# Scan chunk tiles in the place that the level tiles leave, one head group of a hybrid encoder layer

## The chip, the core and the metric

One core of a Trainium2 chip runs one program. Its engines work side by side, each through a queue of its own in a fixed order: TensorE (PE) multiplies, VectorE (DVE), ScalarE (ACT) and GpSimd (POOL) do the elementwise work, and SyncE (SP) issues every DMA of this kernel, one after the other. The metric is the time of one execution on the device in microseconds (us). A profiled execution gives the time of every instruction.

## What is computed

One layer of a bidirectional encoder on 1024 tokens of width 1024, all in float32. Cut to the parts that matter here:

```python
proj = h @ w_in[l]                      # columns for attention, delta net, gate, decays
aq, ak, av, dqkv, dgate, dalpha, dbeta = jnp.split(proj, IN_SPLITS, axis=-1)
attn_o = _window_attention(aq, ak, av, attn_sink[l])     # 8 heads, +-128 tokens
dn_o = _gated_deltanet(dqkv, dgate, ...)                 # 4 heads, both directions
mix = jnp.concatenate([attn_o, dn_o], axis=-1) @ w_out[l]
x = x + _rms_norm(mix, g_mix_post[l])
...                                     # cross-attention into 256 memory tokens, SwiGLU

def step(state, inp):                   # inside the delta net: the scan over chunks
    qg_i, kg_i, u_i, w_i, qk_i, gl_i = inp
    v_new = u_i - jnp.einsum('bhck,bhkv->bhcv', w_i, state)
    o_i = jnp.einsum('bhck,bhkv->bhcv', qg_i, state) + jnp.einsum('bhij,bhjv->bhiv', qk_i, v_new)
    state = state * gl_i[..., None, None] + jnp.einsum('bhck,bhcv->bhkv', kg_i, v_new)
    return state, o_i
```

## The kernel before

**Stages.** The program is a chain of stages. Lists of short codes give the order in which their pieces are written; a scheduler then orders the instructions on each engine when the program is built, and each engine runs them in that order. ORDER_1 projects keys, queries and values of the delta net, convolves them and prepares their chunk products. ORDER_2 (line 38) holds the attention projections (A, V), the gate projections (G), the levels (L, one for each of the four delta-net heads) and the first attention windows (W). ORDER_3 (line 39) holds the norm of the memory tokens (M), the scan steps of both head groups (s01), windows (W), the key products of the memory (K, line 941) and its value products (V, line 954). The output projection `w_out` follows (line 1098), then cross-attention and the feed-forward part.

**Matmuls in three passes.** Weights are loaded as float32 (`wraw`, line 122), cast to a high part on ACT (`whi`, line 103) and subtracted to a low part on DVE or POOL (`wlo`, line 104); three matmuls make one product. `wraw`, `whi` and `wlo` have two buffers each.

**Levels.** `levels(h)` (line 556) solves the triangular systems of one head by blocks. It works in tiles of the pool `tl` (line 743: cz, cw, m5, c5, c6, L5, L6, D5, D6, Z0, Z1, Ul and small ones) and stores Z0 and Z1 to `d_pz` (line 628), from where the scans read them. Two halves of one head run through each other.

**Windows.** `window(n, g)` (line 632) is attention of 128 tokens for four heads: load `qr` (643), scores `psw` on PE (654), the maximum on DVE (656), exponentials on ACT (663), scaling by 1/sum on DVE or ACT (672 or 674); then, in the second half, transposes `ptw` (680), high and low parts `ph` and `pl` (103, 104), the product with the values `pow` (685), and the store of `ao` to `d_mix` (688 to 690). `psw` and `ptw` share two PSUM banks.

**Scans.** `scan(g)` (line 795) is a generator for one head group (two heads, two directions), eight steps. In each step it loads a chunk's `kv` (two DMAs of 512 KB, line 824) and `pz` (two of 256 KB, line 825), multiplies (line 809, PSUM tiles `psc`), makes the corrected values, the new state S and the output `of` or `ol`; the second four steps also load a gate tile and store `osq` to `d_mix` (line 906). The output projection loads `d_mix` as `mraw` (line 1094).

**Where the tiles lie.** Pools are stacks on two sides of the on-chip memory. On the left: `wp` (weights), `sm`, `tw` (windows), then `tl`. On the right: `ra`, then in ORDER_2 the pools of `p1` (`hx` with the normalised input, `trp` with the tiles `rop` and `gt`), and after `p1.close()` (line 787) in the place of these the pool `t3` of the scans (line 793). `tl` is entered in `p1`, so it is closed there, and `mk` (line 914: the memory's norm and its operand `mT`) then stands where `tl` stood. A new tile must wait until the last access to the tiles that lay in its place.

**Chunk tiles.** Even steps ("near") take `pz` from `ra` (tag `rr`) and, for group 0, `kv` from `ra` (tag `sct`). All the rest lies in `t3`: `pz` of the odd steps and `kv` of group 0's odd steps one buffer each, `kv` of group 1 two buffers. A `pz` tile takes 4 KB and a `kv` tile 8 KB of a partition.

Of the kernel before, what the change touches and what calls it, by code (L numbers as in the profile page):

```python
# [10 lines left out]
F32 = mybir.dt.float32  # L11
# [8 lines left out]
P = 128  # L20
# [14 lines left out]


ORDER_1 = ("k0 k1 E0 K0 U0 E1 K1 U1 S0 q0 v0 q1 C0 v1 E2 C1 k2 E3 k3 q2 K2 U2 v2 K3 U3 S1 q3 C2 v3 C3 B0 B1").split()
ORDER_2 = "L0 L1 A4 V A0 A1 G0 G1 L2 L3 W W W A2 A3 G2 G3 W".split()
ORDER_3 = ("M " + "s01 W K " * 5 + "s01 K " * 3 + "s01 V V").split()


# [35 lines left out]
def tile_hybrid_block(  # L77
# [11 lines left out]
    if dump is None:  # L89
        def dump(name, ap):  # L90
            pass
# [17 lines left out]
    def pool(name, bufs, **kw):  # L109
        return tc.tile_pool(name=name, bufs=bufs, reuse_waits="tile", **kw)  # L110
# [26 lines left out]
    p12 = ExitStack()  # L137
# [8 lines left out]
    ra = p12.enter_context(pool("ra", 1, side="right"))  # L146
    p1 = ExitStack()
# [196 lines left out]
    G = sm.tile([P, 2, 4, NT], F32, name="G")  # L344
# [33 lines left out]
    sct = ra.tile([P, 2, S], F32, tag="sct", name="sct")  # L378
# [350 lines left out]
    def issue(order, table):  # L729
        for o in order:  # L730
            table[o[0]](*(int(c) for c in o[1:]))
# [8 lines left out]
    tw = p12.enter_context(pool("tw", 2))  # L740
    tw.tile([P, 384], F32, tag="sc", name="sc", bufs=8)
    vhl = tw.tile([P, NT + 1, 2, 2, 64], F32R, tag="vhl", name="vhl", bufs=1)[:, 0:NT]
    tl_ = p1.enter_context(pool("tl", 2))

    def pair():
        t = ra.tile([P, 2, HALF], F32, tag="rr", name="rr", bufs=2)
# [35 lines left out]
            nc.scalar.activation(gt, pp[hf], AF.Silu)  # L782
            nc.sync.dma_start(d_gate[h * P:(h + 1) * P, hf * HALF:(hf + 1) * HALF], gt)

    issue(ORDER_2, {"A": attn_proj, "V": value_proj, "G": gate_proj, "L": levels, "W": next_windows})
    dump("d_q", d_q); dump("d_k", d_k); dump("d_gate", d_gate)
    p1.close()
    pgs.close()
# [6 lines left out]
    def scan(g):  # L795
# [5 lines left out]
        def tl(name, shape=QUAD, **kw):  # L801
            return t3.tile(shape, F32, tag=f"{name}{g}", name=name, **kw)
# [9 lines left out]
        for step in range(NT):  # L812
# [1 line left out]
            cs = (step, NT - 1 - step)  # L814

            near = step % 2 == 0
            pz = (ra.tile([P, 2, 2, 2, P], F32, tag="rr", name="pz", bufs=2) if near else tl("pz", [P, 2, 2, 2, P], bufs=1))
            if g == 0:
                kv = (ra.tile([P, 2, 2, 4, P], F32, tag="sct", name="kv") if near else tl("kv", [P, 2, 2, 4, P], bufs=1))
            else:  # L820
                kv = tl("kv", [P, 2, 2, 4, P])
            before = loaded
            for d in range(2):
                loaded = nc.sync.dma_start(kv[:, d], d_kv[g][cs[d]])
# [129 lines left out]
    def next_values():  # L954
# [12 lines left out]
        for t in range(2):  # L967
            vv = mk.tile([P, 512], F32, tag="cv", name="vv", bufs=2)
            nc.scalar.copy(vv, pp[t])
            nc.sync.dma_start(d_mv[t, :, ch * 512:(ch + 1) * 512], vv)  # L970

    scans = [scan(g) for g in range(2)]

    def scan_step(pairs):
# [23 lines left out]
    L0 = ExitStack()  # L998
# [84 lines left out]
    L1 = ExitStack()  # L1083
# [29 lines left out]
    L2 = ExitStack()  # L1113
# [63 lines left out]
    L3 = ExitStack()  # L1177
# [13 lines left out]
    def turned_k(xn, k):  # L1191
        pt = pn.tile([P, 512], F32, tag="pn", name="ptn")
        for j in range(4):
            nc.tensor.transpose(pt[:, j * P:(j + 1) * P], xn[j][:, k * P:(k + 1) * P], ident)  # L1194
        return pt
# [8 lines left out]
    for k in range(HK):  # L1204
        p0, p1 = turned_k(xn, k), turned_k(xn, k + HK)
# [32 lines left out]
    for e in range(EARLY):  # L1238
        f = 2 * e
        sg = te.tile([P, 512], F32, tag="sg", name="sg0")  # L1240
        w, A = [], []
# [21 lines left out]
    def bank(name):  # L1263
        return pg.tile([P, 512], F32, tag="pg", name=name)
# [60 lines left out]
    for f in (2 * p for p in turns):  # L1325
# [9 lines left out]
        for i, (W1, W22, (S1, S2, S3, S4), _) in enumerate(wts):  # L1335
            a1, v, u = (tg.tile([P, 512], F32, tag=n, name=n, bufs=b_) for n, b_ in (("a1", 1), ("v", 2), ("u", 1)))
            A = None
            if early:
                nc.sync.dma_start(a1, d_m1[f + i])
            else:  # L1340
                A = bank("pA")
# [10 lines left out]
        for i, (W1, W22, (S1, S2, S3, S4), _) in enumerate(wts):  # L1352
            A, D_, E_, v = st[i]
# [101 lines left out]
    A = [bank("pdA") for _ in range(4)]  # L1455
# [104 lines left out]
```

## Time and profile before

| | |
|---|---|
| runs | 1535.87, 1537.51, 1537.88 us |
| median of the runs | 1537.51 us |
| span of the profiled execution | 1537.6 us |
| PE busy | 1481.4 us (96%), 7451 matmuls |
| DVE busy | 1067.1 us (69%) |
| ACT busy | 743.3 us (48%) |
| POOL busy | 374.6 us (24%) |
| moved by DMA | 242.95 MB, mean 158 GB/s |

The span runs from the first to the last instruction of the profiled execution. A busy share is an average over all stages; a stage has to be read on its own, by a table of its stretch of time or by the instructions in order of time. "Idle before" in such a row is the time for which the engine had nothing to run, and the name after the arrow is what ended it.

### The profile page before, as it was taken

Reading aid. Unit: us, or ns where it says so; the run is one execution under the profiler, and the core shown is the slowest. Engines: PE = TensorE matmul, PEld = TensorE weight load, DVE = VectorE, ACT = ScalarE, POOL = GpSimd, SP = SyncE. Lnnn points to the kernel's source line nnn. Section 1 sums busy time; section 2 is a strip of 40 time slices with the busy share of each in tenths; the row PEclk is TensorE's granted clock in tenths of the full one; section 3 lists DMA queues with packets and bytes.
Section 4 is the critical chain, followed back from the end, with each engine's and each line's share of the span. In section 5 each row is a group of like instructions: output and inputs, shape, how many; then the busy total and the mean of one; then the engine's idle time right before and its main releaser. Section 6 shows DMA issues by size and latency. Waiting matters only on the chain. (4 is left out here: it accounts for less than half of the span.)

```text
span 1537.6 us, 21036 instructions
## 1 busy us (share of the span) xinstructions
PE 1481.4 (96%) x7451; PEld 1246.6 (81%) x7451; DVE 1067.1 (69%) x1732; ACT 743.3 (48%) x1518; POOL 374.6 (24%) x364
## 2 busy tenths in 40 slices
PE   6999999998999899999999999999999999999997
PEld 5888888787999777888888877888888888888786
DVE  6868999686788776534346387776877555696665
ACT  6578732457457665454336564323223333354532
POOL 2020210111247103253102232443433432000021
PEclk9999999999999999999999999999999999999999
DMA  6244575856997665454213354343533334853355
GB/s 207 76 116 139 156 188 155 197 173 166 309 321 219 216 208 195 138 165 136 69 55 138 104 198 130 123 130 110 171 124 96 110 104 161 291 185 96 103 176 166
DMA packets 264710, 242.95 MB, mean 158 GB/s; under 512 B 33801, under 2 KB 203678, under 8 KB 264606
## 3 DMA queue, kind: packets, MB, share of 16 engines
q1 hardware_dynamic: 264605, 241.62, 50.4%
q8 instruction: 58, 0.95, 0.3%
q14 instruction: 47, 0.38, 0.1%
HBM read 172.07 MB, written 66.88 MB: 155 GB/s over the span
## 5 line engine op out<-in xcount | busy, mean ns | idle before, releaser
L103 ACT CAST whi<-wraw 128x1024 fp32r<-128x1024 f32 x108 | 113.4, 1051 | 154.8 <-issue 31.7
L261 PE MATMUL pg<-hlo,whi 128*128 128x512 f32 x352 | 139.5, 397 | 0.0
L261 PE MATMUL pg<-hhi,whi 128*128 128x512 f32 x352 | 139.2, 396 | 0.0
L261 PE MATMUL pg<-hhi,wlo 128*128 128x512 f32 x352 | 138.5, 394 | 0.0
L104 POOL TENSOR_TENSOR wlo<-wraw,whi 128x1024 fp32r<-128x1024 f32 x38 | 91.7, 2414 | 178.7 <-ACT whi L103 169.4
L104 DVE TENSOR_TENSOR wlo<-wraw,whi 128x1024 fp32r<-128x1024 f32 x70 | 87.1, 1245 | 58.6 <-ACT whi L103 54.6
L1052 PE MATMUL pmg<-whi,b 128*128 128x512 f32 x384 | 119.0, 394 | 0.4 <-ACT b L103 0.4
L1231 PE MATMUL pA<-s,whi 128*128 128x512 f32 x352 | 109.3, 392 | 1.0 <-ACT m L1248 1.0
L1052 PEld LDWEIGHTS pmg<-whi,b 128*128 128x128 f32 x384 | 71.4, 188 | 15.3 <-ACT b L103 1.3
L1421 PE MATMUL pdX<-dhl,whi 128*128 128x512 f32 x264 | 76.1, 390 | 1.5 <-ACT dhl L103 0.8
L1231 PEld LDWEIGHTS pA<-s,whi 128*128 128x128 f32 x352 | 65.5, 188 | 14.7 <-ACT m L1248 1.5
L261 PEld LDWEIGHTS pg<-hhi,whi 128*128 128x128 f32 x352 | 66.5, 189 | 13.4 <-ACT hhi L103 0.2
L261 PEld LDWEIGHTS pg<-hhi,wlo 128*128 128x128 f32 x352 | 66.5, 189 | 12.9
L261 PEld LDWEIGHTS pg<-hlo,whi 128*128 128x128 f32 x352 | 66.4, 189 | 12.8
L1052 PE MATMUL pmg<-wlo,b 128*128 128x512 f32 x192 | 71.9, 391 | 0.0
L1308 POOL TENSOR_TENSOR act<-act,up 128x512 f32<-128x512 f32 x33 | 50.1, 1520 | 88.6 <-DVE up L1307 53.2
L103 ACT CAST whi<-araw 128x1024 fp32r<-128x1024 f32 (+1 forms) x36 | 35.4, 982 | 71.4 <-PE pdX L1421 27.6
L1231 PE MATMUL pA<-s,wlo 128*128 128x512 f32 x176 | 68.6, 391 | 0.8 <-DVE wlo L104 0.7
L104 DVE TENSOR_TENSOR wlo<-araw,whi 128x1024 fp32r<-128x1024 f32 (+1 forms) x36 | 40.8, 1133 | 38.5 <-ACT whi L103 38.4
L286 DVE SCALAR_TENSOR_TENSOR acc<-cp,cols,acc 128x1024 f32<-128x1024 f32 x48 | 62.1, 1296 | 0.1
L1280 POOL TENSOR_TENSOR sr<-wraw 128x512 f32<-128x512 f32 x22 | 30.6, 1392 | 127.0 <-DMA wraw<-in_w_gate_up_dram 125.8
L1451 POOL TENSOR_SCALAR frs<-sq 128x1 f32<-128x1 f32 x8 | 12.0, 1497 | 195.9 <-ACT jk L1440 195.0
(415 smaller groups left out, 4097.9 us busy)
## 6 DMA issues: line engine op xcount, KB each, us to landing
wraw<-in_w_gate_up_dram SPq DMA_DIRECT2D x52, 512.0 KB, 3.8
kv<-d_kv SPq DMA_DIRECT2D x32, 512.0 KB, 6.9
wraw<-in_w_in_dram SPq DMA_DIRECT2D x22, 512.0 KB, 5.6
b<-in_w_down_dram SPq DMA_DIRECT2D x20, 512.0 KB, 7.0
araw<-d_as SPq DMA_DIRECT2D x20, 512.0 KB, 3.9
pz<-d_pz SPq DMA_DIRECT2D x32, 256.0 KB, 5.3
wraw<-in_w_ckv_dram SPq DMA_DIRECT2D x16, 512.0 KB, 8.7
wraw<-in_w_out_dram SPq DMA_DIRECT2D x16, 512.0 KB, 4.0
```

The costliest lines, as they stand in the source:

```text
L103: nc.scalar.copy(hi, src)
L104: (eng or nc.vector).tensor_tensor(lo, src, f32(hi), ALU.subtract)
L261: nc.tensor.matmul(p_, w[:, k, :], ah[a][:, k, :], start=(k == 0 and i == 0), stop=(k == nk - 1 and i == 2))
L286: nc.vector.scalar_tensor_tensor(acc, cp[:, t:t + S], taps[t], acc, ALU.mult, ALU.add)
L1052: nc.tensor.matmul(pp[t], act[a][:, k, tt], w_[:, kk, :], start=(k == 0 and i == 0), stop=(k == KT - 1 and i == 2))
L1231: nc.tensor.matmul(out_, w[a][:, k, :], xx[b_][:, k, :], start=(start and k == 0 and i == 0), stop=(k == HK - 1 and i == 2), skip_group_ch ...
L1280: nc.gpsimd.tensor_tensor(s[0], b_[:, 0:HK], b_[:, HK:], ALU.add)
L1308: nc.gpsimd.tensor_tensor(o_, o_, up, ALU.mult)
L1421: nc.tensor.matmul(banks[t], a[:, k - k0, tt], w, start=(first and k == 0 and i == 0), stop=(k == NB - 1 and i == 2), skip_group_check=not ...
L1451: nc.gpsimd.tensor_scalar(rs, sq[:, 1, t:t + 1], sq[:, 0, t:t + 1], D * EPS, ALU.add, ALU.add)
```

## The change

`tl` gets an exit stack of its own and is closed by a new entry T in ORDER_2, written after the levels of the last head. In its place on the left a pool `tk` is opened, which stays until the scans end. `pz` of the odd steps, `kv` of group 0's odd steps and both buffers of `kv` of group 1 now come from `tk` (4 + 8 + 4 + 16 = 32 KB of a partition) and not from `t3`. The number of buffers of each stays the same.

```diff
-ORDER_2 = "L0 L1 A4 V A0 A1 G0 G1 L2 L3 W W W A2 A3 G2 G3 W".split()
+ORDER_2 = "L0 L1 A4 V A0 A1 G0 G1 L2 L3 T W W W A2 A3 G2 G3 W".split()
...
-    tl_ = p1.enter_context(pool("tl", 2))
+    ptl = ExitStack()
+    tl_ = ptl.enter_context(pool("tl", 2))
+    tk = []
+
+    def scan_chunks():
+
+        ptl.close()
+        tk.append(p12.enter_context(pool("tk", 2)))
+
...
-    issue(ORDER_2, {"A": attn_proj, "V": value_proj, "G": gate_proj, "L": levels, "W": next_windows})
+    issue(ORDER_2, {"A": attn_proj, "V": value_proj, "G": gate_proj, "L": levels, "W": next_windows, "T": scan_chunks})
...
             near = step % 2 == 0
-            pz = (ra.tile([P, 2, 2, 2, P], F32, tag="rr", name="pz", bufs=2) if near else tl("pz", [P, 2, 2, 2, P], bufs=1))
-            if g == 0:
-                kv = (ra.tile([P, 2, 2, 4, P], F32, tag="sct", name="kv") if near else tl("kv", [P, 2, 2, 4, P], bufs=1))
+            pz = (ra.tile([P, 2, 2, 2, P], F32, tag="rr", name="pz", bufs=2) if near else
+                  tk[0].tile([P, 2, 2, 2, P], F32, tag=f"pz{g}", name="pz", bufs=1))
+            if g == 0 and near:
+                kv = ra.tile([P, 2, 2, 4, P], F32, tag="sct", name="kv")
             else:
-                kv = tl("kv", [P, 2, 2, 4, P])
+                kv = tk[0].tile([P, 2, 2, 4, P], F32, tag=f"kv{g}", name="kv", bufs=1 + g)
```

## The prediction

> **What bounds the kernel now.** I read the page's head first, then a table of stretches of time, then the instructions in order inside the stretches where TensorE idles.
>
> ```profile
> span 1537.6 us, 21036 instructions
> ...
> PE 1481.4 (96%) x7451; PEld 1246.6 (81%) x7451; DVE 1067.1 (69%) x1732; ACT 743.3 (48%) x1518; POOL 374.6 (24%) x364
> ```
>
> PE leaves 1537.6 - 1481.4 = 56.2 us idle. The change adds and removes no instruction, so it can gain only PE idle time or PE clock. The table of windows (columns: stretch, then busy time of PE, PE weight load, DVE, ACT, POOL; granted PE clock; DMA share; GB/s) shows where some of it lies:
>
> ```profile
> 355.00:366.00 11.00, 10.92 (x63) 9.05 (x61) 5.95 (x15) 8.41 (x19) 2.38 (x4) 1.00 0.72 203
> 366.00:387.00 21.00, 14.14 (x95) 11.76 (x96) 14.77 (x36) 15.60 (x34) 3.23 (x6) 0.96 0.88 222
> 387.00:396.00 9.00, 9.00 (x54) 8.81 (x54) 4.40 (x13) 2.32 (x5) 2.18 (x2) 0.72 1.07 324
> 396.00:444.00 48.00, 47.90 (x400) 46.86 (x399) 43.13 (x127) 23.32 (x55) 14.76 (x10) 1.00 1.01 315
> 444.00:516.00 72.00, 65.52 (x519) 62.46 (x518) 59.95 (x153) 54.84 (x169) 41.56 (x55) 1.00 0.70 215
> 516.00:553.00 37.00, 32.05 (x152) 25.26 (x153) 28.36 (x54) 23.75 (x42) 1.69 (x3) 1.00 0.81 289
> 553.00:580.00 27.00, 27.00 (x132) 22.54 (x132) 18.12 (x29) 17.02 (x30) 0.20 (x1) 1.00 0.51 166
> 580.00:600.00 20.00, 19.13 (x84) 15.17 (x83) 10.52 (x10) 8.31 (x11) 0.00 (x0) 1.00 0.50 167
> ```
>
> The start of the scans (366 to 387) has 21.00 - 14.14 = 6.86 us of idle PE. Behind it stands a stretch at clock 0.72: 0.28 x 9 + 0.04 x 21 = 3.4 us of work lost. From 444 to 516 the idle time is 6.48 us, in the V stage (516 to 553) 4.95. These are the only places that the change touches: the two programs have one instruction order before some 365 us and again from about 585 us, and PE is nearly full in the stage that follows, so that what is won or lost by 585 moves the end by as much.
>
> Why PE starves at 366 is seen on SP's queue, then on PE and ACT (start, busy time, engine, line, operation; in brackets the idle time before it and what ended it):
>
> ```profile
> 363.42 0.34 SPq L825 DMA_DIRECT2D pz<-d_pz  x1
> 369.02 0.33 SPq L783 DMA_DIRECT2D d_gate<-gt  x1
> 369.45 1.33 SPq L824 DMA_DIRECT2D kv<-d_kv  x3
> 373.00 0.54 SPq L126 DMA_DIRECT2D wraw<-in_w_ckv_dram  x1
> 385.57 0.33 SPq L824 DMA_DIRECT2D kv<-d_kv  x1
> ```
>
> ```profile
> 369.54 1.06 PE L809 MATMUL psc<-kv,pz 128*128 128x128 f32 x8
> ...
> 374.58 0.68 PE L809 MATMUL psc<-kv,pz 128*128 128x128 f32 x4 [0.97 <-ACT mT L106]
> ...
> 386.68 0.80 PE L949 MATMUL pck<-mT,whi 128*128 128x256 f32 x2 [3.54 <-ACT whi L103]
> ...
> 395.66 0.48 PE L949 MATMUL pck<-mT,whi 128*128 128x256 f32 x2
> ```
>
> SP stands from 363.76 to 369.02 at the store of the last gate tile. Behind it are the chunk loads of group 1 and the first weight of the memory's keys, issued at 373.00; it is cast on ACT only at 385.58 (below), 12.6 us later, beside a DMA share of 0.88. PE then waits 3.54 us, and the half-speed stretch begins.
>
> **The change, part by part.** *Opening and closing pools* issues nothing, and the buffers of each tag are as many: 0, hidden by nothing because there is nothing to hide.
>
> *Chunk loads earlier.* With the tiles no longer in the gate's pool, the first two steps' loads (ten DMAs) stand ahead of the gate store, so they can go at about 363 and not from 369.45: 6 to 7 us earlier. That moves past one store and delays it by ten issues of about 0.4 us (1.33 for three), some 4 us; nobody reads the gate tile before the scan's second half.
>
> *The memory's norm later.* This is what the change gives away. `mk` now lies above `tk` and reaches into the place of the gate's tiles, so the two squares must wait for the last gate activation and stand behind it on ACT; the transposes ptm and the first scan step come on PE behind all scores of windows 4 and 5. Before, the squares ran ahead of the gate:
>
> ```profile
> 363.81 1.05 ACT L924 ACTIVATE mjk<-mt 128x1024 f32<-128x1024 f32 x1
> ...
> 367.10 1.28 ACT L782 ACT_TABLE_LOAD   x1
> 368.39 0.60 ACT L782 ACTIVATE gt<-pg 128x512 f32<-128x512 f32 x1
> ...
> 385.58 1.04 ACT L103 CAST whi<-wraw 128x1024 fp32r<-128x1024 f32 x1 [1.79 <-DMA wraw<-in_w_ckv_dram]
> ```
>
> The first weight load waits for these transposes, since `wraw` holds the memory tokens until then, and so do the chunk products of step 0. So I walk the new order to its first key product. ACT is the engine that sets it. Rows of the groups by line and shape (busy time and mean ns, 355 to 400):
>
> ```profile
> L663 ACT ACTIVATE sc<-sc,nm 128x384 f32<-128x384 f32 x12 | 7.2, 607 | 0.0
> L103 ACT CAST ph<-ptw 128x512 fp32r<-128x512 f32 x9 | 5.0, 582 | 1.7 <-PE ptw L680 1.7
> L106 ACT ACTIVATE mT<-ptm,cols 128x256 fp32r<-128x256 f32 x8 | 3.4, 478 | 2.0 <-PE ptm L934 2.0
> L688 ACT COPY ao<-pow 64x512 f32<-64x512 f32 x2 | 1.2, 583 | 2.7 <-PE pow L685 2.7
> L846 ACT COPY vn<-psc 128x512 f32<-128x512 f32 x2 | 1.2, 578 | 0.0
> L103 ACT CAST khi<-kraw 128x1024 fp32r<-128x1024 f32 x1 | 1.0, 1048 | 0.0
> ```
>
> From about 364.6 on ACT runs eight casts of 0.58 (4.7), two table loads of 1.28 (2.6), the gate (0.6), two windows' exponentials of 4 x 0.61 (4.8) with their sums (0.4), two squares and their sums (2.3), two `ao` copies (1.2), two `qs` casts (1.2), eight `mT` (3.4), two `vn` (1.2) and two weight casts (2.1): 24.5 us. I add 4.2 us of waits, an estimate: 1.4 for the first ptw behind the scores, 2.5 for ptm (the group's old wait was 2.0), 0.3 elsewhere. That is 393.3, and PE reaches its first key product at about 395, with some 7 us of window work ahead of the old place. In the old run the same amount of PE work was done at about 395.4 to 395.6, just before the last row of PE above. Term: **-0.4**. Bounds: if the loads and not ACT set it, ACT's 4.2 us of waits shrink to 1, -3.6; if the transposes queue twice as long, +2.
>
> Here a rule of the Trainium skill bears. The largest PE gap of my walk is 3.0 us. In the trace a gap of 3.54 us was followed by clock 0.72. "TensorE: Matmul & The Clock Gate", section "What's actually happening", says that the clock halves after a whole idle window of about 3.4 us; the 3.54 row agrees, and by it the walk keeps the full clock. The same page's "Part 4: PE-mode transpose" says that transposes don't count as busy in the same way; the new sparse stretch holds many. By that the loss of clock would return; it is a rival below.
>
> *The scan and key stages, 396 to 516.* Up to 444 PE is 47.90 of 48 busy and DMA at 1.01: the order inside it costs nothing, covered by PE. After 444 PE waits in short gaps, the first being
>
> ```profile
> 446.98 0.50 PE L685 MATMUL pow<-ph,vhl 128*128 128x512 f32 x1 [1.95 <-ACT ph L103]
> ```
>
> a window's product behind a late cast. With windows ahead half of this may go: **-1.0**, between 0 and -1.95. The other 4.5 us are the scan's own chain of dependences and stay.
>
> *The V stage, 516 to 553.* In the new order of ACT two of the casts `s<-mraw` stand ahead of the second value weight and all four ahead of the third; the four x tiles and the norm weight move behind the weights on SP. Before:
>
> ```profile
> 519.16 1.05 ACT L103 CAST whi<-wraw 128x1024 fp32r<-128x1024 f32 x1 [3.92 <-PE pcv L965]
> ...
> 522.24 1.05 ACT L103 CAST whi<-wraw 128x1024 fp32r<-128x1024 f32 x1 [0.99 <-PE pcv L965]
> ...
> 526.30 1.05 ACT L103 CAST whi<-wraw 128x1024 fp32r<-128x1024 f32 x1
> ...
> 529.75 1.05 ACT L103 CAST s<-mraw 128x1024 fp32r<-128x1024 f32 x1 [0.31 <-DMA mraw<-d_mix]
> ...
> 536.37 1.04 ACT L103 CAST whi<-wraw 128x1024 fp32r<-128x1024 f32 x1 [0.62 <-DMA wraw<-in_w_ckv_dram]
> ```
>
> The mraw loads wait for the last `osq` stores, so the second weight's cast comes near 529.75 - 1 + 2 x 1.05 = 530.9, some 8.6 us late; the third near 534, some 8 late. Queued behind them on ACT are window 7's exponentials and `ph`, and PE's value products wait. Bounds of the new idle time: 0 (window work covers all) and 8.6 (nothing covers). My walk of the PE rows in between leaves 0.9 + 1.2 + 0.9 + 1.6 + 0.8 = 5.4, an estimate. The old idle time, 4.95, was in part the casts of late weights (PE's two largest gaps), and SP issued x tiles ahead of weights:
>
> ```profile
> 537.47 1.19 PE L965 MATMUL pcv<-whi,mT 128*128 128x512 f32 x4 [1.65 <-ACT whi L103]
> ...
> 544.92 1.19 PE L965 MATMUL pcv<-whi,mT 128*128 128x512 f32 x4 [1.23 <-ACT whi L103]
> ```
>
> ```profile
> 525.16 0.50 SPq L1062 DMA_DIRECT2D xr<-in_x_dram  x1
> 526.27 3.72 SPq L1062 DMA_DIRECT2D xr<-in_x_dram  x3
> ```
>
> SP spends 0.5 + 3.7 = 4.2 us on four x tiles; behind the weights they let these land earlier, and the old gaps go. Term: 5.4 - 4.95 = **+0.5**; ends -4.95 and +5.4.
>
> *The output projection.* Its idle time from 580 to 600 is 0.87 us, one late weight cast:
>
> ```profile
> 596.98 1.21 PE L1052 MATMUL pmg<-whi,s 128*128 128x512 f32 x4 [0.86 <-ACT whi L103]
> ```
>
> With window work done earlier ACT is freer there: **-0.9**, or 0. The x tiles, now loaded behind, are covered by 27.00 of 27 us of busy PE at a DMA share of 0.51; late, they would stall the residual, not PE.
>
> Sum: 1537.6 - 0.4 - 1.0 + 0.5 - 0.9 = 1535.8. Three of the four terms can be larger on the gain's side before they meet a bound, the first above all (-3.6 against -0.4), so I put the forecast one below, at **1535**. The profiled span is 0.1 from the runs' median, 1537.51, so no correction is due.
>
> **The rivals.** *The late loads were the whole stall.* For it: SP stood 5.2 us, and everything that starved at 369 to 386 was behind. Then PE has the old amount of work done by 392 instead of 395.5, at full clock, -3.6, and with the other terms -2 to -4 more: 1530.5. Against: ACT has 24.5 us of work in that stretch, whatever the loads do.
>
> *ACT stands at mraw in the V stage.* The slower side. In-order ACT waits for the mix loads with weight casts behind it; new idle 5.4 us, while the old 4.95 stay, because they had ACT's load as a cause and not the x tiles: 1537.6 + 5.4 - 0.4 = 1542.6. It decides if mraw lands more than some 6 us after the first value weight's cast; before it was 529.75 - 519.2 = 10.5. Against: PE's gaps of 1.65 and 1.23 there wait for weight casts, the first of them behind a weight's DMA (the row at 536.37), which gets the queue earlier.
>
> *The clock falls again.* A gap over 3.4 us at ptm gives the 3.4 us back: 1535 + 3.4 = 1538.4, no change.
>
> **How the numbers follow.** Forecast 0.38 (own range 1532 to 1538), early loads 0.22, ACT at mraw 0.34, clock 0.06. About 0.2%, 3.1 us, is what a measurement here can tell from no change: faster means below 1534.4. Of the forecast's 0.38 I put 0.20 there, since the terms lean to the gain, and 0.18 within. Faster 0.20 + 0.22 = 0.42; same 0.18 + 0.06 = 0.24; slower 0.34. The range 1530 to 1543 takes in both outer rivals' values and leaves out 0.1 on each side, for bounds met together.
>
> **What the profile would show.** Group 1's chunk loads issued near 363, ahead of the gate store; squares behind the gate; ACT over 85% busy from 366 to 392; the first key product near 395; no clock below 0.95 from 366 to 400. In the V stage the casts of mraw ahead of the second value weight, and PE idle time near 5 us from 516 to 553. I am wrong if the first key product comes before 391 or after 398, if a clock row near 0.7 remains, or if the V stage idles over 8 us.

## The result, and the profile after

| | before | after |
|---|---|---|
| median of the runs on one chip | 1536.69 us (4 runs, 1535.56 to 1537.88) | 1545.01 us (4 runs, 1543.78 to 1545.70) |
| ratio to before, 95% interval | 1 | 1.0046 (1.0034 to 1.0059) |
| span of the profiled execution | 1537.6 us | 1543.0 us |
| PE idle from 366 to 600 us | 19.2 us | 15.7 us |

The changed kernel is slower by some 0.46%, 7 us of 1537 (the two medians lie 8.3 us apart). The forecast was 1535, the range ended at 1543. More runs on another chip gave 1.0037 (1.0025 to 1.0050).

The table of windows of the changed kernel, in the stretches that the prediction used (stretch, busy us of PE, weight load, DVE, ACT, POOL, PE clock, DMA share, GB/s):

```profile
366.00:387.00 21.00, 16.48 (x81) 11.86 (x79) 16.62 (x43) 15.18 (x32) 4.58 (x8) 0.84 0.72 256
387.00:396.00 9.00, 6.03 (x26) 5.03 (x27) 6.41 (x16) 7.80 (x19) 2.36 (x1) 0.64 0.67 146
396.00:444.00 48.00, 46.07 (x371) 44.48 (x371) 40.87 (x109) 24.04 (x56) 14.59 (x10) 1.00 0.94 305
444.00:516.00 72.00, 71.78 (x586) 70.04 (x585) 63.45 (x169) 49.62 (x151) 38.39 (x49) 1.00 0.75 233
516.00:553.00 37.00, 31.52 (x151) 25.32 (x149) 26.93 (x55) 20.42 (x47) 5.35 (x8) 0.91 0.63 204
553.00:580.00 27.00, 26.41 (x116) 21.75 (x117) 15.39 (x20) 15.60 (x26) 0.00 (x0) 0.94 0.71 248
580.00:600.00 20.00, 20.00 (x90) 16.57 (x89) 13.85 (x13) 12.19 (x17) 0.00 (x0) 1.00 0.64 231
```

Read as PE work done at full speed (busy time by clock) and compared with the rows of before, this is: from 366 to 444, 63.8 us of work against 68.0, so 4.2 us lost; from 444 to 516, 71.8 against 65.5, so 6.3 won back; in the V stage and behind it (516 to 580), 53.5 against 59.1, so 5.5 lost; from 580 to 600, 0.9 won. Net: 2.6 us less work done by 600 us. Another 1.8 us of the 5.4 between the two spans were there already at 360, where both programs still run the same instructions (the last product of the levels starts at 360.0, before at 358.2); the profiled executions of the experiments, with the same order up to there, scatter by nearly 4 us at that point, so these aren't taken for the change's.

Such sums are rough: the mean clock of a stretch isn't the clock of its busy time, and a product that runs alone counts longer than one in a row (in e4 below each of 80 transposes takes 272 ns, and all together 8.9 us). Both kernels run the same 7451 products, so PE's progress can also be counted by the columns that its products have streamed. By this count, an estimate from the traces (a column of the scans and transposes at the price that e4's 8.9 us give, one of the split products at half of it), the changed kernel is behind the kernel before by 1.5 us at 366, 8.8 at 444, 1.2 at 516, 6.4 at 580 and 5.0 at 600. Other prices move the 8.8 between 7.5 and 9.2 and the rest by 0.2. What the front lost was made up by 516, and the V stage lost it again.

What the change was to do, it does. SP of the changed kernel:

```profile
364.68 1.03 SPq L833 DMA_DIRECT2D kv<-d_kv  x2
...
372.38 0.32 SPq L791 DMA_DIRECT2D d_gate<-gt  x1
...
387.03 0.54 SPq L126 DMA_DIRECT2D wraw<-in_w_ckv_dram  x1
```

The chunk loads go at 364.68, ahead of the gate store, and not at 369.45. But the first key weight goes at 387.03 and not at 373.00, for the reason that ACT and PE show (timeline rows of the changed kernel):

```profile
369.26 0.60 ACT L790 ACTIVATE gt<-pg 128x512 f32<-128x512 f32 x1
...
377.83 1.06 ACT L933 ACTIVATE mjk<-mt 128x1024 f32<-128x1024 f32 x1
...
392.17 1.10 ACT L103 CAST whi<-wraw 128x1024 fp32r<-128x1024 f32 x1
```

```profile
382.60 0.66 PE L943 MATMUL ptm<-ident,mt 128*128 128x128 f32 x4
383.09 1.06 PE L817 MATMUL psc<-kv,pz 128*128 128x128 f32 x8
...
399.91 0.48 PE L958 MATMUL pck<-mT,whi 128*128 128x256 f32 x2
```

The squares of the norm came at 377.83 (before 363.81), the first scan product at 383.09 (before 369.54, a row of the prediction), the first key product at 399.91 (before 386.68). All of it is 13 to 14 us later.

### The profile page after: what moved, and what is told of

Read it like the earlier page. It is cut to its first block, busy times and chain, and to the rows that moved or that the text cites. A ratio compares the mean times of both kernels' runs of the same rounds, so it can differ in the third digit from the quotient of the medians.

```text
span 1543.0 us, 21042 instructions
## 1 busy us (share of the span) xinstructions
PE 1489.4 (97%) x7451; PEld 1252.1 (81%) x7451; DVE 1072.1 (69%) x1732; ACT 741.5 (48%) x1518; POOL 374.7 (24%) x364
## 5 line engine op out<-in xcount | busy, mean ns | idle before, releaser
L104 DVE TENSOR_TENSOR wlo<-wraw,whi 128x1024 fp32r<-128x1024 f32 x70 | 87.0, 1244 | 65.5 <-ACT whi L103 61.4
L1240 PEld LDWEIGHTS pA<-s,whi 128*128 128x128 f32 x352 | 65.5, 188 | 14.8 <-ACT m L1257 1.5
L1430 PEld LDWEIGHTS pdX<-dhl,whi 128*128 128x128 f32 x264 | 49.3, 188 | 12.7 <-issue 1.1
```

What stands on the lines that cost most here:

```text
L104: (eng or nc.vector).tensor_tensor(lo, src, f32(hi), ALU.subtract)
L1240: nc.tensor.matmul(out_, w[a][:, k, :], xx[b_][:, k, :], start=(start and k == 0 and i == 0), stop=(k == HK - 1 and i == 2), skip_group_ch ...
L1430: nc.tensor.matmul(banks[t], a[:, k - k0, tt], w, start=(first and k == 0 and i == 0), stop=(k == NB - 1 and i == 2), skip_group_check=not ...
```

## The experiments

Every build orders its instructions anew, so most edits move more than they name; that is said where it matters. Ratios are to the kernel before, run beside it on the same chip. "In the trace" means the profiled execution of that run. The theories' letters change their sense on the way: in e1 and e2 theory S is the V stage; from e9 on S is the start of the scans and V the V stage.

### Is it the clock?

Three more half-clock stretches stand in the changed kernel's trace than in before's. The first runs took the change apart and tried the clock.

**e1_kv1_only.** Only group 1's kv comes from `tk`, so that `tk` and `mk` fit into the place of the level tiles.

```diff
-            pz = (ra.tile(...) if near else tk[0].tile(..., tag=f"pz{g}", name="pz", bufs=1))
+            pz = (ra.tile(...) if near else tl("pz", [P, 2, 2, 2, P], bufs=1))
-            if g == 0 and near: ...
+            if g == 0: kv = (ra.tile(...) if near else tl("kv", [P, 2, 2, 4, P], bufs=1))
-            else: kv = tk[0].tile(..., tag=f"kv{g}", bufs=1 + g)
+            else: kv = tk[0].tile(..., tag="kv1", bufs=2)
```

> Only kv of group 1 (16 KB) is taken from tk; the odd steps' pz and group 0's odd kv go back to t3. tk (16 KB) and mk (20 KB) then fit together into the 40 KB of the level tiles, so the memory's norm need not wait for the gate. Theory C (clock): the half-clock stretches decide the time; each window of 3.41 us at half clock costs 1.7 us. With the norm early the two stretches at 376 and 389 should shrink to at most one: 1536 to 1539, and time minus 1.7 us per half-clock window should be the same as for the kernels before and after (about 1533). Theory S (V stage): the casts of mraw ahead of the value weights cost the time whatever the start of the scans does: about 1542 if they stand there again.

Measured: 1540.03 us, ratio 1.0007 (0.9991 to 1.0022). The early loads of group 1 are there (364.86 in the trace), the norm is early too, and the kernel is as fast as before. So the loss goes, and the early loads bring nothing that can be measured in the time. In the trace they do bring something: by the count of columns PE is 2.1 us behind before at 366, 4.5 ahead at 516, and 0.3 behind at 580, so the V stage takes it back. The loss goes although one mraw cast stands ahead of the fourth of the V stage's eight weights and all four ahead of the fifth (in the changed kernel two and four; the prediction, counting from the cast at 519.16, which is the third, called these weights the second and the third). Here the scan ends at 515.5.

**e2_odd_only.** The other half: odd pz and group 0's odd kv from `tk`, group 1's kv from `t3`.

```diff
-                kv = tk[0].tile([P, 2, 2, 4, P], F32, tag=f"kv{g}", name="kv", bufs=1 + g)
+                kv = tl("kv", [P, 2, 2, 4, P])     # group 1
```

> The other half: the odd steps' pz and group 0's odd kv come from tk (16 KB), kv of group 1 stays in t3 behind the gate. Early loads are lost for group 1, the norm stays early. Theory C: the start of the scans looks like that of the kernel before, with one stretch of two half-clock windows near 385, 1536 to 1538. Theory L (loads decide): as before, 1537, and at least 4 us slower than the run with only kv of group 1 in tk. Theory S: 1542 if the mraw casts stand ahead of the value weights.

Measured: 1546.38 us, 1.0041 (1.0024 to 1.0059). Neither expectation of about 1537 held; theory S's 1542 comes nearest (the ratio makes 1543 of 1537), and two of mraw's casts do stand ahead of the fifth value weight, all four ahead of the sixth. With group 1's kv late, PE stands at it in the trace:

```profile
385.54 1.22 PE L817 MATMUL psc<-kv,pz 128*128 128x128 f32 x4 [2.94 <-DMA kv<-d_kv]
```

Loads behind the gate can cost, then. In the kernel before, whose loads are behind the gate too, PE waits only 0.3 us for kv from 366 to 400.

**e3_warm.** Four matmuls ahead of the transposes of each of six blocks, whose result the transposes overwrite.

```diff
             pp = pw.tile([P, 512], F32, tag="pw", name="ptw")
+            if g * NT + n in WARM:           # WARM, NWARM = (3, 4), 4
+                for _ in range(NWARM):
+                    nc.tensor.matmul(pp, vhl[:, k0 + j, g]..., keys[g][0][:, 0:512], start=True, stop=True)
```

> The changed kernel with 4 additional matmuls of 512 columns ahead of the transposes of each of 6 blocks of windows 3 and 4 (24 in all, 5.5 us of PE work if none of it falls in idle time); their result is overwritten by the transposes. Theory C: PE is busy in more of the windows at 372 and 386, the clock stays at 1.00 there, 6.8 us come back and 0 to 3 us are spent: 1538 to 1541. Theory I (the idle time and the order cost, the clock only goes along): 1545 to 1550.

Measured: 1553.1 us, 1.0087 (1.0057 to 1.0117). The clock did stay at 1.00 from 366 to 400, and three half-clock stretches appeared at 425, 562 and 589. Theory C's 1538 to 1541 did not come although the clock stayed up, but another order stands behind the edit, and the time is at the end of theory I's range by the ratio (1550 beside 1537) and above it as measured. It tells little between them.

**e4_transposes.** 80 transposes and, a turn later, 40 matmuls of 512 columns inside the full feed-forward part of the kernel before.

```diff
+            if f == 2 * turns[9] and i == 0:
+                with tc.high_priority(5000):
+                    for q in range(80):
+                        nc.tensor.transpose(B_[:, (q % 4) * P:(q % 4 + 1) * P], ident, ident)
+            if f == 2 * turns[10] and i == 0:
+                with tc.high_priority(5000):
+                    for q in range(40):
+                        nc.tensor.matmul(B_, S2[0][:, 0, :], T2[0][:, 0, :], start=True, stop=True)
             product(B_, S2, T2)
```

> The kernel before with two blocks added on PE in the feed-forward part, where it is full and at clock 1.00: 80 transposes of 128 columns one behind the other (about 8.8 us) and, a turn later, 40 matmuls of 512 columns (about 9.1 us); both write a bank that the next product overwrites. If transposes count as busy for the clock: clock 1.00 in and behind both blocks, 1536.7 + 18 = 1554.6. If they count for nothing: clock near 0.5 from 3.4 to 6.8 us after the block's start on, the later transposes take twice as long, the products behind too: 1558 to 1563, and nothing of the kind at the block of matmuls.

Measured: 1560.17 us, 1.0131 (1.0098 to 1.0164), 20 us more for 18 us of work. The time alone doesn't decide, since the two answers lay as little as 3.4 us apart; the trace does. Its rows are the transposes' own, then the windows over the first block, the time behind it and the second block:

```profile
L1348 PE MATMUL pB<-ident x80: 272/273/273, 1239.8 to 1248.4; 128*128 128x128 f32 x80
```

```profile
1239.00:1248.50 9.50, 9.50 (x86) 9.29 (x84) 9.50 (x12) 2.99 (x5) 4.48 (x3) 1.00 0.33 97
1248.50:1256.00 7.50, 7.50 (x35) 6.21 (x34) 2.49 (x3) 0.89 (x2) 2.54 (x2) 1.00 0.57 195
1286.00:1296.00 10.00, 10.00 (x46) 8.29 (x45) 9.72 (x12) 2.84 (x5) 4.36 (x3) 1.00 0.38 116
```

The clock is 1.00 through 8.9 us of nothing but transposes, and they take 272 or 273 ns each. These transposes count as busy.

**e5_after_again.** The changed kernel itself, once more, with more executions.

> The changed kernel unchanged, for more executions beside the kernel before on one chip. The traces so far show that the clock is granted in a fixed grid of 3.41 us whose place is another in each execution, so both kernels should scatter by several times 1.7 us. Theory C (clock): the changed kernel is slower by 3 to 8 us in the middle, and its trace at full clock (span less the work lost to half clock) is again near 1527.6, some 3 us less than the kernel before's 1530.8. Theory I (idle time and order): it is slower by 8 us in every execution, and the span less the clock's loss is longer than before's.

Measured: 1545.88 us (1543.65 to 1548.11), 1.0037 (1.0025 to 1.0050). Five executions of five are slower than the median before, although some half-clock stretches lie elsewhere in this trace (523.6 to 527.0, 544.0 to 547.4). Less the time lost to half clock ahead of the end, its span is 1530.4 us: not theory C's 1527.6, and not longer than the 1530.8 of before, as theory I had it. The run doesn't decide between them.

**e6_fill_two** and **e7_fill_four.** Matmuls in the idle gaps of the changed kernel: five in each of the two at 375 and 386; in e7 also five in the gap at 521 and five in the gap at 551.65, both by a weight of zeros.

```diff
+            for _ in range(5 if (g * NT + n, j) == (3, 2) else 0):      # into ptw's bank, ahead of the transposes
+                nc.tensor.matmul(pp, vhl[...], keys[0][0][:, 0:512], start=True, stop=True)
...
+            for _ in range(5 if (g * NT + n, j) == (4, 0) else 0):      # into pow's bank, ahead of its first product
+                nc.tensor.matmul(po, vhl[...], keys[0][0][:, 0:512], start=True, stop=True)
...
+                for _ in range(5 if (g * NT + n, j, i) == (12, 2, 1) else 0):   # e7
+                    nc.tensor.matmul(po..., zero, ph, start=False, stop=False)
...
+            for _ in range(5 if (ch, kp) == (1, 2) else 0):             # e7
+                nc.tensor.matmul(pp[0], zero, mT[0][...], start=False, stop=False)
```

> The changed kernel with 5 matmuls of 512 columns (1.1 us, overwritten by the next product) in the gap that began at 374.95 and 5 in the one that began at 386.3; the order of all other instructions is the same but for a dozen matmuls. Theory C: the windows at 372 and 386 come out over 0.6 busy, both stretches go, and the time falls by up to 6.8 us against the changed kernel in the same call, though the other stretches move about. Theory I: the time is the same or up to 2.3 us longer.

> As the run before, with 5 further matmuls (by a weight of zeros, so they add nothing) in the gap at 521 and 5 ahead of the product that stood at 551.65. Theory C: no half-clock window between 365 and 600, the granted clock is below 1.00 only at 285 and at the end: 1533 to 1536, 7 to 12 us less than the changed kernel in the same call. Theory I: the changed kernel's time plus 0 to 4.5 us.

Measured: e6 1545.49 us, 1.0034 (1.0022 to 1.0047); e7 1545.44 us, 1.0042 (1.0029 to 1.0055). The windows of e7:

```profile
366.00:387.00 21.00, 16.96 (x92) 12.32 (x91) 16.31 (x44) 15.75 (x35) 4.59 (x8) 1.00 0.77 268
387.00:396.00 9.00, 6.34 (x36) 5.43 (x35) 6.01 (x16) 7.77 (x18) 2.12 (x1) 0.81 0.66 145
396.00:444.00 48.00, 45.07 (x365) 43.50 (x364) 41.64 (x108) 23.39 (x56) 14.81 (x11) 1.00 0.91 297
...
516.00:553.00 37.00, 33.36 (x173) 26.89 (x172) 28.54 (x58) 22.81 (x57) 4.29 (x8) 1.00 0.66 204
```

Three of the four stretches are gone in e7 (one of 3.4 us is left near 392), in e6 those at 376 and 553, and the time is that of the changed kernel beside them, 1545.88. PE runs faster and waits longer instead: from 387 to 396 it is busy 6.34 us at clock 0.81, filler included, where it was 6.03 at 0.64. The scan starts and ends where it did (383.3 and 526.4 in e7; 383.1 and 526.3). The 20 fillers of e7 are up to 4.4 us of work themselves (1.1 for five), so this doesn't price the clock to the microsecond; but e6, with half as many and nearly the changed kernel's order, gives the same time. Half clock beside a wait for ACT or DVE costs almost nothing here. Theory C falls as the explanation of the 7 us.

**e8_fill_all.** As e7, with nine more in the gap of 3.42 us that both kernels have at 283.

> As the run before, with 9 more matmuls (2 us) in the gap of 3.42 us that stands at 283 in both kernels; the order behind it is another one than the changed kernel's in some 600 places. Theory C: no stretch at 285 either: 1530 to 1534, less than both kernels, if the new order leaves no new sparse window. Theory I: 1545 or more.

Measured: 1559.11 us, 1.0117 (1.0100 to 1.0135). Its order differs in 600 places; in the trace PE is idle 6.8 us from 560 to 600. It says nothing on the clock, and much on what another order can cost.

### Is it the start of the scans, or the V stage?

**e9_late_scan.** The kernel before; on PE alone, the first scan products are queued behind the scores of window 5.

```diff
             pv = bank()
-            mm(pv, pz[:, :, :, 1, :], R)
+            with ExitStack() as order_:
+                if step == 0: order_.enter_context(tc.issue_after(scores[23].ins))
+                mm(pv, pz[:, :, :, 1, :], R)
```

> The kernel before with one order added on PE: the first product of each scan's first step is queued behind the last scores of window 5 (the memory's norm and all loads stay as early as they were). Theory S (the scan's chain): in the runs so far the scan takes some 144 us from its first to its last product whatever PE does beside it, and about 130 us pass from there to the first query product of the cross-attention, so the time follows the moment of the first scan product (369.5 us before, 383.1 after). Here that should be near 383, and the time 3 to 7 us above the kernel before's: 1542 to 1546. Theory N (what costs is the late norm, with the weights behind it) and theory C (clock): 1536 to 1541, the kernel before's own spread.

**e10_late_norm.** The kernel before; on ACT, the norm's squares are queued behind the last gate activation.

```diff
-            nc.scalar.activation(jk, mt, AF.Square, accum_out=ss)
+            with tc.issue_after(gates[-1].ins):
+                nc.scalar.activation(jk, mt, AF.Square, accum_out=ss)
```

> The kernel before with the two squares of the memory's norm queued on ACT behind the last gate activation, without any of the changed tiles: the wait that the change adds, alone and in a milder form (4 places later on ACT, not 14). Theory S: the first scan product comes 3 to 6 us later, the time is 1 to 4 us longer: 1538 to 1543. Theory N: the same sign. If neither holds and the place of the tiles itself matters: 1537 to 1540, as before.

**e11_swap.** The changed kernel; the norm comes to lie over `hx`, not over the gate's tiles.

```diff
-    hx = p1.enter_context(pool("hx", 1, side="right"))
     trp = p1.enter_context(pool("trp", 2, side="right"))
+    hx = p1.enter_context(pool("hx", 1, side="right"))
```

> The changed kernel with the pools trp (gate tiles) and hx (normalised input) in the other order, so that the memory's norm comes to lie over hx, which is free earlier, and not over the gate's tiles. All early chunk loads stay. Theory S: the first scan product comes near 374 and not 383, and the changed kernel's loss of 5 us mostly goes: 1538 to 1541. Theory V (casts of mraw ahead of the value weights in the V stage; they stand there here too): 1543 to 1546.

**e12_hold.** The changed kernel; ACT's casts of mraw are queued behind the copy that ends the V stage's first half.

```diff
-            split(mxT[hf][0][:, k2, :], mxT[hf][1][:, k2, :], raw[:, k2, :])
+            with tc.issue_after(vcopy[1 if hf == 0 else 3].ins):
+                split(mxT[hf][0][:, k2, :], mxT[hf][1][:, k2, :], raw[:, k2, :])
```

> The changed kernel with one order added on ACT and DVE: the casts of mraw are queued behind the copy of the memory values that ends the first half of the V stage, so the value weights' casts come first as in the kernel before. The scan's start is the changed kernel's, 383. Theory S: 1543 to 1546, as the changed kernel. Theory V: 1538 to 1541.

Measured, with the first scan product, the last one's start (a transpose of `ol`) and the first score of the cross-attention (`pcs`) in the trace, and how far PE is behind the kernel before by the count of columns (estimates, as above). The last four rows ran on a chip of their own, with a median of 1537.82 before, so the ratios are to be compared and not the medians. The traced execution of e11 is its fastest, 1536.64.

| kernel | median us | ratio, 95% | scan from | to | first `pcs` | behind at 516 | at 580 |
|---|---|---|---|---|---|---|---|
| before | 1536.69 | 1 | 369.5 | 516.3 | 661.6 | 0 | 0 |
| after | 1545.01 | 1.0046 (1.0034 to 1.0059) | 383.1 | 526.3 | 666.7 | 1.2 | 6.4 |
| e9_late_scan | 1545.26 | 1.0043 (1.0027 to 1.0060) | 390.9 | 528.2 | 669.3 | 2.1 | 9.0 |
| e10_late_norm | 1544.02 | 1.0045 (1.0030 to 1.0060) | 374.9 | 525.2 | 667.2 | -0.6 | 7.1 |
| e11_swap | 1540.79 | 1.0015 (1.0000 to 1.0030) | 371.3 | 520.6 | 659.5 | -2.3 | -0.6 |
| e12_hold | 1540.22 | 1.0008 (0.9992 to 1.0023) | 382.4 | 526.5 | 661.9 | 1.5 | 1.7 |

The start of the scan and the first `pcs` of e12 come from these two lines of its tiles, first and last start behind the durations:

```profile
L817 PE MATMUL psc<-kv,pz x128: 270/275/377, 382.4 to 507.7; 128*128 128x128 f32 x128
...
L1148 PE MATMUL pcs<-kr,b x192: 277/283/365, 661.9 to 850.7; 128*128 128x256 f32 x192
```

e9 shows that an edit that makes the first scan product late is enough for the whole loss in the kernel before (it comes at 390.9, later than the 383 that was aimed at); e10 that the wait behind the gate is enough too. e11 takes the norm off the gate's tiles and gives two thirds of the loss back. So the start of the scans matters, as theory S said. But e10 starts its scan only 5 us late, 3.6 of which its trace has already at 360, and loses as much, and e12 starts it at 382.4, where the changed kernel does, and has the loss mended: 526.5 at the scan's end, as the changed kernel, and 5.0 us less from there to `pcs` (135.4, not 140.4). Theory S alone doesn't hold. In every kernel of the table PE is within some 2 us of the kernel before at 516, and the three with the full loss lose it between 516 and 580. Both e9 and e10 also have all four casts of mraw ahead of the fifth value weight, where the kernel before has them behind it. The trace of e12 against that of the changed kernel shows what its edit moved. ACT's casts and DVE's subtractions in the V stage, changed kernel:

```profile
532.46 1.05 ACT L103 CAST s<-mraw 128x1024 fp32r<-128x1024 f32 x1 [0.78 <-DMA mraw<-d_mix]
...
535.07 1.04 ACT L103 CAST whi<-wraw 128x1024 fp32r<-128x1024 f32 x1
538.41 2.00 ACT L103 CAST s<-mraw 128x1024 fp32r<-128x1024 f32 x2
540.78 1.06 ACT L103 CAST whi<-wraw 128x1024 fp32r<-128x1024 f32 x1
...
552.49 1.04 ACT L103 CAST whi<-wraw 128x1024 fp32r<-128x1024 f32 x1 [4.21 <-DMA wraw<-in_w_ckv_dram]
```

```profile
540.28 2.35 DVE L104 TENSOR_TENSOR s<-mraw,s 128x1024 fp32r<-128x1024 f32 x2
543.15 1.21 DVE L104 TENSOR_TENSOR wlo<-wraw,whi 128x1024 fp32r<-128x1024 f32 x1
```

and e12:

```profile
538.85 1.05 ACT L103 CAST whi<-wraw 128x1024 fp32r<-128x1024 f32 x1 [1.29 <-DMA wraw<-in_w_ckv_dram]
...
545.98 1.06 ACT L103 CAST whi<-wraw 128x1024 fp32r<-128x1024 f32 x1
```

```profile
539.93 1.23 DVE L104 TENSOR_TENSOR wlo<-wraw,whi 128x1024 fp32r<-128x1024 f32 x1 [0.73 <-ACT whi L103]
```

With mraw's split ahead of it, the same weight (the fifth) is subtracted at 543.15 and not at 539.93. Only then is its `wraw` buffer free, and the load of the seventh goes at 544.68 and not at 541.32; its cast comes at 552.49 and not at 545.98. Of these 6.5 us, 3.4 are the late issue; the others are the landing, 7.8 us from issue to cast against at most 4.7 in e12.

One other wait stood in the same place: SP of the changed kernel waits 4.4 us at the load of `mkr`, ahead of those weights. Three more runs asked whether it was that.

**e13_mkr_late.** That load alone is queued behind the last value weight.

```diff
-        nc.sync.dma_start(raw, src)
+        with tc.issue_after(last_value_load.ins):
+            nc.sync.dma_start(raw, src)
```

> The changed kernel with one order added on SP: the load of mkr is queued behind the last value weight's load. In the changed kernel it stands ahead of the last two of these and waits 4.4 us for DVE's split of mraw. The order of the casts on ACT stays the changed kernel's. Theory Q (SP's queue stands at mkr): the product that stood at 551.65 to 553.59 comes some 4 us earlier, 1539 to 1541. Theory A (ACT stands at the mraw casts): 1543 to 1546, as the changed kernel.

Measured: 1544.9 us, 1.0046 (1.0029 to 1.0063): theory Q falls. In the trace SP now waits for the buffer itself and issues the weight at 544.74, as before the edit. But it lands earlier without `mkr` ahead of it:

```profile
544.74 1.83 SPq L128 DMA_DIRECT2D wraw<-in_w_ckv_dram  x2
```

```profile
549.74 1.05 ACT L103 CAST whi<-wraw 128x1024 fp32r<-128x1024 f32 x1 [1.39 <-DMA wraw<-in_w_ckv_dram]
```

The cast of the seventh weight is 2.75 us earlier than in the changed kernel (552.49), and the time is the same. So the 4.21 us wait for that weight, taken by itself, is not the price either.

**e14_swap_mkr** and **e15_swap_hold** add e11's pool order to e13 and to e12.

> As the run before, with the pools of the gate tiles and of the normalised input in the other order, so that the norm comes earlier (first scan product near 372). Theory S (the moment of the first scan product counts even where the V stage is in order): 1534 to 1537, faster than the kernel before. If the scan's start is worth nothing by itself: 1538 to 1541.

> The other pool order together with the mraw casts queued behind the first half's copy of the memory values. Theory S: 1534 to 1537. If neither the early loads nor the earlier start is worth anything: 1538 to 1541.

Measured: e14 1539.47 us, 1.0015 (1.0000 to 1.0031); e15 1542.94 us, 1.0030 (1.0017 to 1.0043). Both have the early loads and an early start (373.4 and 371.8), and neither beats the kernel before. The forecasts by theory S, 1534 to 1537, fall; e14 is in the other range, 1538 to 1541, and e15 above both. The two mends don't add up: e15 comes out slower than either of its parts (1.0015 and 1.0008), though the intervals overlap. In its build five of the eight value weights come ahead of mraw's casts, as in the kernel before, and not six as in e12; its scan ends at 524.0.

Taken together, the full loss shows where the scan ends late and mraw's casts stand ahead of the fifth or sixth value weight (after 526.3, e2 525.0, e9 528.2, e10 525.2). It doesn't show where the scan ends early (e1, 515.5) or where the casts are moved back behind the sixth (e12). e11 (520.6) lies between; e14 (527.0, casts ahead of the fifth, 1.0015) fits worst: by the count of columns it is 4.0 us behind at 516 and at 580, while e13 goes from 0.7 to 7.8 and e15 from 1.0 to 4.8. Why the V stage of e14 loses nothing stays open. No version of this change was found that is faster than before.

## Why the prediction was wrong, step by step

**Chunk loads earlier: right, and worth nothing in the time.** They moved ahead of the gate store, by 4.8 us. In e1, where they come without the late norm, the ratio is 1.0007 (0.9991 to 1.0022). The rival "the late loads were the whole stall" is out: it gave 1530.5.

**The norm later: seen, and priced too low.** The walk gave the first key product "at about 395", with 7 us of window work ahead, and -0.4 for it all. It came at 399.91. The work on ACT was about right (the first weight cast was to be done by 393.3 and began at 392.17), though ACT was 78% busy from 366 to 392 and not over 85%. What failed is taking ACT's end for PE's: PE came to the key product without a wait, through products queued ahead of it, the first scan product was 13.5 us late, and by 444 PE was 4.2 us of work behind by the rows, 7.3 more than at 366 by the count of columns. The step said of the stretch to 444 that "the order inside it costs nothing, covered by PE", from PE busy 47.90 of 48. That was wrong by 444 and right by 516: PE had made it up. In e12 the same late start costs nothing that can be measured in the end.

**Clock: the walk's rule was wrong, and it hardly mattered.** "The largest PE gap of my walk is 3.0 us", so the clock would hold. It fell four times, in or beside gaps of 2.46, of 1.70 and 1.19, of 2.70 and of 1.93 us. By the clock rows alone the price would be 8 us more than before; e6 and e7 show that most of it lies beside waits.

**Scan and key stages: -1.0 forecast, -6.3 measured** (444 to 516). The direction was right, the bound of -1.95 was not: the 4.5 us called the scan's own chain, which "stay", went too. PE had the late work of the front to fill the gaps, and idled 0.22 us.

**V stage: the step that failed and decided the sign.** The term was +0.5: 5.4 us of new waits less the old 4.95, because the weights would land earlier with the x tiles behind them "and the old gaps go". They did not go: 5.5 us of work were lost from 516 to 580 (5.2 by the count of columns). Of these, 1.1 are idle time (6.06 against 4.95, so the size of the idle time was met, 5.48 from 516 to 553 where "near 5" was said) and 4.4 half clock, for which the term had nothing. Yet in e7, without half clock there, PE was 1.9 us further at 580, idled 1.73 from 580 to 600 (the changed kernel 0.00), and was as far behind at 600 (5.1 and 5.0): there, what PE waits for set the time, and not its speed.

The slower rival had the place (mraw ahead of the weight casts) and nearly the price (5.4, and 1542.6 for the whole). e12 bears it out: mraw's splits moved behind the sixth weight, and the ratio falls from 1.0046 to 1.0008. Its condition was wrong, and so was its "first" value weight (the cast at 519.16 is the third). ACT waited only 0.8 us for mraw to land in this trace; the splits themselves take 4 us on ACT and 5 us on DVE, ahead of the fifth weight's subtraction, and the load behind that one is 3.4 us late. By which of these delays the time is lost stays open: e13 takes 2.75 us from the last of them and gains nothing.

**Output projection: -0.9, as forecast.**

The front's loss and the V stage's, 4.2 and 5.5, less the 6.3 and 0.9, give 2.6 us by 600 in this trace (3.5 by the count of columns); with the 1.8 us that were there at 360 the latter comes near the 5.4 between the spans. The runs show 7, which two single executions can't give to the microsecond. The two places aren't independent: mending either gives most of the 7 us back. That a scan that ends 10 us later leaves less other work for PE in the V stage, so that delayed weights are no longer covered, would explain e12 and e11, but e14, with the scan's end at 527.0, speaks against it. How much belongs to which place stays open, and so do e14, e15 and e8's loss.

## What to carry to other kernels

A tile that moves takes its old neighbours' waits with it: here 12 KB of the memory's norm came to lie on the gate's tiles (32 KB of `tk` and 20 of `mk`, where the level tiles had 40), and that wait put a new order on the stages behind it, while the loads that the change freed brought nothing to the time. Before pricing a new order stage by stage, follow a loss to the end: the front's was made up some 70 us later, and the one that stayed came in the stage where splits stood ahead of weights with two buffers. A long wait for a load that stands out in a trace need not be the price: e13 shortened it and gained nothing. And a half-speed row is a price only where PE is what others wait for; fill the gap and see before blaming the clock.

## What the runs showed of the hardware

The clock is granted in a fixed grid. In the changed kernel it falls at 375.89, 389.54, 522.66 and 553.38 us; these lie 4, 39 and 9 steps of 3.413 us apart. In all 17 traces the falls behind 100 us fit such a grid to 0.01 us, whose place is another one in each execution, which may be one source of the runs' scatter (1533.2 to 1541.8 for the kernel before on one chip); that isn't shown. Grid windows of the changed kernel, twice one at full clock and the one at half clock behind it, and two of before that did not bring a fall:

```profile
372.48:375.89 3.41, 1.96 (x10) 1.09 (x9) 1.48 (x2) 3.37 (x7) 1.06 (x2) 1.00 1.02 389
375.89:379.30 3.41, 1.89 (x4) 1.25 (x5) 1.87 (x6) 3.41 (x10) 0.23 (x1) 0.50 1.05 386
...
519.25:522.66 3.41, 1.59 (x8) 0.86 (x6) 3.41 (x10) 2.70 (x11) 0.63 (x1) 1.00 0.27 75
522.66:526.07 3.41, 2.27 (x7) 2.05 (x8) 3.03 (x8) 0.58 (x1) 1.80 (x3) 0.50 0.54 183
```

```profile
443.26:446.67 3.41, 1.78 (x16) 1.58 (x15) 1.11 (x5) 1.79 (x3) 0.67 (x1) 1.00 1.05 396
446.67:450.08 3.41, 3.10 (x23) 2.94 (x24) 3.00 (x7) 3.23 (x12) 3.18 (x3) 1.00 0.95 266
```

Between 30 and 1520 us of the 17 traces, a window at full clock in which PE was busy under 48% was followed by half clock 48 times of 48; between 48 and 60%, 14 times of 47 (the 57% of 372.48 was, the 52% of 443.26 was not); above 60%, 6 times of some 7200. So an idle stretch of 3.4 us isn't needed, an idle share of about half a window is enough, and where the window begins counts. The 3.54 us gap of before, which the prediction read as one idle window, lies across two windows; the one that brought the fall, from 381.82 to 385.23, had PE busy 38%. The Trainium skill ("TensorE: Matmul & The Clock Gate", "What's actually happening") speaks of a whole idle window; the trace disagrees, and its remark that transposes don't count as busy the same way ("Part 4: PE-mode transpose") is not what the 80 transposes of e4 show, which are float32 and stand in the trace as matmuls.
